# Modulation rows on VectorE behind single up tiles of the feed-forward

## The chip, the cores and the metric

The kernel runs on one core of a Trainium2 chip (trn2). The metric is the device time of one launch in microseconds; the times given are medians over several runs. A profile is one further execution, taken by the hardware profiler; its span runs from the first instruction to the last.

## What is computed

The reference is two layers of a diffusion trunk over 512 latent tokens and 128 context tokens, 1024 features wide. In each layer a conditioning vector (one for the latent tokens, `c`, and one for the context, `c_ctx`) gives six modulation vectors, a mixer with three groups of heads follows, and then a gated feed-forward with a depthwise convolution of width 3 over the tokens:

```python
def _modulation(cvec, w_ada, b_ada):
    m = jax.nn.silu(cvec) @ w_ada + b_ada
    return jnp.split(m[:, None, :], 6, axis=-1)

def _conv_ffn(h, w_ug, conv_w, conv_b, w_down):
    u = h @ w_ug
    ...
    uc = sum(up[:, i:i + n] * conv_w[i] for i in range(CONV_W)) + conv_b
    a, g = jnp.split(uc, 2, axis=-1)
    return (jax.nn.silu(g) * a) @ w_down
```

`w_ug` is 1024 x 5632, `w_down` 2816 x 1024. All is in float32; a product is made of three matmuls on a high and a low part of each factor.

## The kernel before

Features lie on the 128 partitions and the 640 tokens along the free dimension. Each weight tile of 128 x 1024 is loaded (`wr`), split by ScalarE into its high part (`wh`, line 125) and by VectorE into its low part (`wl`, line 188).

The feed-forward (from line 1268 on) has 22 pairs of up tiles. A pair is one tile of the a half and one of the g half. An up tile is 48 matmuls (8 slices of the contraction, 3 products, 2 halves of the tokens, line 278) into one of two wide PSUM accumulators (`Acc`, pool `mm`, two buffers). After a tile, `conv` (line 1278) works on it: VectorE reads the accumulator into `u` (line 1282, two instructions), ScalarE copies the edges (`u`, line 125, two instructions) and these are the last readers of the accumulator; VectorE makes a small `bb` (line 1286), ScalarE the middle tap `y` (line 1289, two instructions), and VectorE adds the other two taps (line 1292, two instructions). For a g tile there follow Silu on ScalarE (line 1306), the product `z` of both halves on VectorE (line 1311), and its split into `th` (ScalarE) and `tl` (VectorE, line 144).

The pairs come in groups of 6, 6, 6 and 4. Behind the first pair of a group stands the down projection of the group before (`dn`, eight chunks of output features). `u["plan"]` holds this order.

The modulation vectors of later use are made in the background, by VectorE: `ada_dve` (line 350 on) is a generator. Its first step loads and prepares the two conditioning vectors (`sbc`); each later step is a row: POOL's queue loads 128 x 1024 weights (`wa`, line 361, two buffers), and VectorE multiplies them with each vector and sums along the row (line 364, two instructions, output `junk`). Layer 0's generator has 48 rows, layer 1's has 8. `CFG[l]["ada"]` says how many steps are taken behind each pair; in the loop over the plan they follow both callbacks (lines 1339 to 1345). In the first three down groups one further step is taken behind each chunk.

Tiles `u`, `y`, `z`, `th`, `tl` and `junk` come from one pool with one tag, S. The framework's planner puts the instructions of each engine in an order before the run: it starts from the order of the program and may move an instruction ahead where it is ready, except where `pin` keeps the order of the program.

Of the kernel before, what the change touches and what calls it, by code (L numbers as in the profile page):

```python
# [32 lines left out]
CFG = [{}, {}]  # L33
# [1 line left out]
CFG[0]["fill"] = (5.5, 6.0, 8.5, 8.5, 5.5, 3.0, 5.5, 9.5, 5.5, 6.5, 8.0, 7.5, 8.5, 11.0, 5.0)  # L35
CFG[0]["early"] = (0.5, 1.0, 1.0, 1.0, 0.7, 0.0, 0.3, 0.7, 1.0, 0.5, 0.3, 1.0, 0.5, 0.3, 0.5)
CFG[0]["mid"] = (0.5, 0.5, 0.2, 0.5, 0.0, 0.5, 0.0, 1.0, 0.5, 0.5, 0.8, 0.0, 0.0, 1.0, 0.0)
CFG[0]["ada"] = (3, 1, 1, 1, 2, 1, 1, 1, 1, 2, 1, 1, 1, 1, 1, 2, 1, 1, 1, 1)
CFG[0]["ahead"] = (8, 4)
CFG[0]["kv"] = 0  # L40
CFG[0]["late"] = ()
# [6 lines left out]
CFG[1]["fill"] = (7.5, 4.5, 4.5, 8.0, 9.0, 4.0, 5.5, 4.5, 5.0, 7.0, 11.5, 10.5, 10.5, 7.5, 5.0)  # L48
CFG[1]["early"] = (1.0, 0.7, 0.5, 0.7, 0.7, 1.0, 0.7, 0.3, 0.5, 0.7, 0.1, 1.0, 1.0, 0.5, 0.3)
CFG[1]["mid"] = (0.5, 0.8, 1.3, 0.0, 0.0, 0.2, 0.2, 0.2, 0.2, 0.0, 0.0, 0.0, 0.0, 0.0, 0.0)  # L50
CFG[1]["ada"] = (3, 1, 2, 1, 2)
CFG[1]["ahead"] = (4, 5)
CFG[1]["kv"] = 7
CFG[1]["late"] = (3,)
# [24 lines left out]
def hybrid_step(ctx: ExitStack, tc: tile.TileContext, I, O):  # L79
# [10 lines left out]
    def S(name, dt=F32, w=NT):  # L90
        return sp.tile([128, w], dt, tag="S", name=name)
# [23 lines left out]
    def SM(name, w=4, bufs=4):  # L115
        return sm.tile([128, w], F32, tag=name, name=name, bufs=bufs)

    def halves(ap):
        return ap.rearrange("p (a b) -> p a b", a=2)
# [4 lines left out]
    def acopy(out, in_):  # L124
        return nc.scalar.activation(out, in_, AF.Copy)  # L125
# [16 lines left out]
    def hilo(hi, lo, src, fix=False):  # L142
        pin(acopy(hi, src), fix)
        nc.vector.tensor_sub(lo, src, f32(hi))
# [55 lines left out]
    for l in range(L):  # L200
# [6 lines left out]
        for n in CFG[l]["order"].split():  # L207
# [6 lines left out]
            elif n[:2] == "po":  # L214
                i = int(n[2])
# [43 lines left out]
    def P(l, n):  # L259
        return pk[l][:, PK[n][0]:PK[n][1]]  # L260
# [972 lines left out]
    if True:  # L1233
# [22 lines left out]
        for l in range(L):  # L1256
            u = U[l]

            def begun():
                x.clear()  # L1260
                i = nc.vector.tensor_scalar_mul(nsink[:, l], P(l, "sink"), -1.0)
                if l:
                    tc.keep_in_program_order(i)

            xn, nrm = mixer(l, nrm, begun, I["xT"] if l == 0 else xd)


            hs = nrm.hs()
            cv = P(l, "conv").rearrange("p (t q) -> p t q", q=4)
            T = {}  # L1270
            bg = ada_dve(0, [(0, n) for n in range(40, 48)] + [(1, n) for n in range(40)]) if l == 0 else ada_dve(48, [(1, n) for n in range(40, 48)])
            made = 0

            nws = SM("nws", 2 * NFT, 1)
            nc.vector.reduce_sum(out=nws, in_=cv[:, :, 0:3], axis=AX.X)
            nc.vector.tensor_scalar_mul(nws, nws, -1.0)

            def conv(ps, t):
                uu = S("u", w=UW)
                for c0, c1, o, p in ((0, NL, 0, 1), (CX, NT, 256, 515)):  # L1280
                    n = c1 - c0
                    nc.vector.tensor_mul(halves(uu[:, p:p + n]), ps.t[:, :, o:o + n // 2], halves(nrm.r[:, c0:c1]))  # L1282
                for v, o in enumerate((uu[:, 0:514:513], uu[:, 514:644:129])):
                    acopy(o, ps.t[:, 1, HF + v:HF + v + 1].to_broadcast([128, 2]))
                bb = SM("bb", 2)
                nc.vector.scalar_tensor_tensor(out=bb, in0=uu[:, 513:515], scalar=nws[:, t:t + 1], in1=cv[:, t, 3:4].to_broadcast([128, 2]), op0=ALU.mult, op1=ALU.add)  # L1286
                y = S("y", w=UW)
                for v, (c0, c1) in enumerate(((0, 513), (513, TW))):
                    nc.scalar.activation(y[:, c0:c1], uu[:, c0 + 1:c1 + 1], AF.Identity, bias=bb[:, v:v + 1], scale=cv[:, t, 1:2])  # L1289
                yy = y[:, :TW]  # L1290
                for q in (0, 2):
                    nc.vector.scalar_tensor_tensor(out=yy, in0=uu[:, q:q + TW], scalar=cv[:, t, q:q + 1], in1=yy, op0=ALU.mult, op1=ALU.add)  # L1292
                return yy

            ya = {}

            def cb_a(f):
                def go(ps):
                    ya[f] = conv(ps, 2 * f)
                return go  # L1300

            def cb_g(f):
                def go(ps):
                    y = conv(ps, 2 * f + 1)
                    a = ya.pop(f)
                    nc.scalar.activation(y, y, AF.Silu)  # L1306
                    if f == NFT - 1:
                        nc.scalar.activation(SM("root", 1, 1), y[:, 1:2], AF.Sqrt, bias=eps[:, 0:1], scale=0.0)
                    z = S("z")
                    for c0, c1, o in ((0, NL, 0), (CX, NT, 2)):  # L1310
                        nc.vector.tensor_mul(z[:, c0:c1], a[:, c0 + o:c1 + o], y[:, c0 + o:c1 + o])
                    T[f] = tuple(S(n, F32R) for n in ("th", "tl"))
                    hilo(T[f][0], T[f][1], z)
                return go

            fin = l == L - 1
            nxt = Norm(xn, None if fin else l + 1, 0)
            if fin:
                yout = {}

                def hfin(hf, c):
                    if c not in yout:
                        yout[c] = S("yo")
                    sl = slice(hf * HF, (hf + 1) * HF)
                    nc.vector.scalar_tensor_tensor(out=yout[c][:, sl], in0=xn[c][:, sl], scalar=P(0, "gfin")[:, c:c + 1], in1=nxt.r[hf][:, :HF], op0=ALU.mult, op1=ALU.mult)  # L1325
                    nc.sync.dma_start(out=O["y"][c, :, sl], in_=yout[c][:, sl])

            def upd_d(last):
                def go(c, ps, hfs):
                    resid(xn[c], ps, l, 5, c, hfs)  # L1330
                    if last:
                        for hf in hfs:
                            nxt.sq(c, hf)
                        if not fin and 1 in hfs:
                            nc.gpsimd.dma_start(out=xd[c], in_=xn[c])
                return go

            for kind, a in u["plan"]:
                if kind == "up":
                    for q, cb in (("a", cb_a(a)), ("g", cb_g(a))):  # L1340
                        ps = Acc()
                        drain(dense(W.get(u[q, a]), hs, range(8), ps, True, True, n=UW))
                        cb(ps)
                    for _ in range(CFG[l]["ada"][a] if a < len(CFG[l]["ada"]) else 0):
                        made += next(bg, 0)
                    continue
                while made < 8:
                    made += next(bg)
                f0, f1 = GROUPS[a]
                nk = f1 - f0  # L1350
                ts = tuple({k: T[f0 + k][q] for k in range(nk)} for q in range(2))
                last = a == len(GROUPS) - 1
                up = upd_d(last)
                if not last:
                    for c in range(8):
                        ps = Acc()
                        drain(dense(W.get(u["d", a, c]), ts, range(nk), ps, True, True))
                        up(c, ps, (0, 1))
                        next(bg, None)
                else:  # L1360
                    drain(bg)
                    accs = [Acc(), Acc(), Acc(False)]
                    for ks in (range(nk - 1), range(nk - 1, nk)):
                        for c in range(3):
                            drain(dense(W.get(u["dl", c // 2]), ts, ks, accs[c], ks[0] == 0, ks[0] != 0, off=(c % 2) * nk))
                            if ks[0]:
                                up(c, accs[c], (0, 1))
                    ps = Acc()
                    drain(dense(W.get(u["dl", 1]), ts, range(nk), ps, True, True, off=nk))
                    up(3, ps, (0, 1))  # L1370
                    items = [(c, W.get(u["dl", c // 2], 3 - c // 4), range(nk), (c % 2) * nk) for c in range(4, 8)]
                    done = 0
                    for i in tail(nxt, items, ts, up):
                        upto = CFG[l]["next"][i]
                        for c in range(done, upto):
                            if fin:
                                hfin(0, c)
                            else:
                                nxt.h(0, c)
                        done = upto  # L1380
                    if fin:
                        nxt.stats(1)
                        for c in range(done, 8):
                            hfin(0, c)
                        for c in range(8):
                            hfin(1, c)
                for f in range(f0, f1):
                    T.pop(f)
            nrm = nxt
# [123 lines left out]
```

## Time and profile before

| | us |
|---|---|
| median of 3 runs | 1578.85 (1576.09 to 1584.0) |
| profiled execution, its own time | 1582.09 |
| its span | 1580.3 |
| TensorE busy | 1525.2 |
| VectorE busy | 1116.7 |
| ScalarE busy | 712.3 |

Times in the profile are microseconds from the start of the span. PE is TensorE, DVE is VectorE, ACT is ScalarE, POOL is GpSimd. L278 is line 278 of the kernel; a name like `u<-mm` is the output and the input by the program's names. A trailing x2 says that two instructions in a row are merged. Idle time in square brackets is followed by what ended it. An instruction can be shown to end after the next one on its engine has begun, so what an instruction takes of its engine is read from start to start.

### The profile page before, as it was taken

What the parts mean: (1) busy time and instruction counts of PE and PEld (TensorE: products, weight loads), DVE (VectorE), ACT (ScalarE), POOL (GpSimd) and SP (SyncE); (2) the same over time, 40 slices, a digit from 0 to 9 for tenths busy, and PEclk for the clock granted to TensorE, in tenths of its full rate; (3) what the DMA queues carried; (4) which work ended last, traced back from release to release, by engine and by line L of the source; (5) the groups of instructions that cost most, each with busy time, mean ns of one, the idle gap of its engine ahead of it and who ended that gap; (6) DMA issues with size and microseconds to landing.
All of it is one profiled execution on the core that took longest, in us unless ns stands there. A gap on an engine that the chain in (4) does not pass through costs nothing. (4 is left out here: it accounts for less than half of the span.)

```text
span 1580.3 us, 25827 instructions
## 1 busy us (share of the span) xinstructions
PE 1525.2 (97%) x10082; PEld 1426.3 (90%) x10082; DVE 1116.7 (71%) x2257; ACT 712.3 (45%) x1403; POOL 103.7 (7%) x225
## 2 busy tenths in 40 slices
PE   9999989899999999999999999989999999999997
PEld 7977775599999999999999887869999999999997
DVE  5765674477897888889778777867885466466366
ACT  4555664564432432441445666646433243244142
POOL 1200111100000000001011000120000000000000
PEclk9999999899999999999999999999999999999998
DMA  9542239113334335235244202331332222221211
GB/s 363 166 145 74 73 98 312 56 54 120 116 124 169 120 104 196 104 104 193 81 142 133 72 25 86 114 142 54 120 99 75 81 74 61 94 77 52 100 54 67
DMA packets 61800, 177.59 MB, mean 112 GB/s; under 512 B 7360, under 2 KB 9856, under 8 KB 61680
## 3 DMA queue, kind: packets, MB, share of 16 engines
q1 hardware_dynamic: 44112, 116.41, 22.1%
q0 software_dynamic: 17568, 59.55, 11.2%
q8 instruction: 79, 1.29, 0.3%
q14 instruction: 41, 0.34, 0.1%
HBM read 165.02 MB, written 10.91 MB: 111 GB/s over the span
## 5 line engine op out<-in xcount | busy, mean ns | idle before, releaser
L278 PE MATMUL mm<-hh,wh 128*128 128x320 f32 x1632 | 377.5, 312 | 12.3 <-ACT u L125 9.1
L278 PE MATMUL mm<-hl,wh 128*128 128x320 f32 x1632 | 377.2, 310 | 0.7 <-DVE hl L486 0.4
L278 PE MATMUL mm<-hh,wl 128*128 128x320 f32 x1632 | 376.9, 310 | 0.0
L125 ACT ACTIVATE wh<-wr 128x1024 fp32r<-128x1024 f32 (+2 forms) x189 | 185.9, 984 | 343.1 <-PE mm L278 263.9
L278 PEld LDWEIGHTS mm<-hh,wh 128*128 128x128 f32 x1632 | 273.8, 188 | 20.6 <-ACT u L125 11.0
L278 PEld LDWEIGHTS mm<-hl,wh 128*128 128x128 f32 x1632 | 275.6, 188 | 4.0 <-issue 2.1
L278 PEld LDWEIGHTS mm<-hh,wl 128*128 128x128 f32 x1632 | 274.5, 188 | 3.3 <-issue 3.3
L188 DVE TENSOR_TENSOR wl<-wr,wh 128x1024 fp32r<-128x1024 f32 (+2 forms) x187 | 210.9, 1128 | 48.2 <-ACT wh L125 47.3
L1292 DVE SCALAR_TENSOR_TENSOR y<-u,pk,y 128x642 f32<-128x642 f32 x176 | 156.2, 887 | 67.9 <-ACT y L1289 64.2
L278 PE MATMUL mm<-th,wh 128*128 128x320 f32 x656 | 152.4, 310 | 0.0
L278 PE MATMUL mm<-th,wl 128*128 128x320 f32 x656 | 152.2, 309 | 0.0
L278 PE MATMUL mm<-tl,wh 128*128 128x320 f32 x656 | 152.0, 309 | 0.0
L537 DVE SCALAR_TENSOR_TENSOR x<-mm,mod,x 128x192 f32<-128x192 f32 (+2 forms) x222 | 84.9, 435 | 70.6 <-PE mm L278 70.6
L364 DVE CUSTOM_DVE_ANT_0 junk<-wa,sbc 128x1024 bf16<-128x1024 f32 x112 | 132.1, 1223 | 1.8 <-DMA wa<-in_wat 1.8
L1289 ACT ACTIVATE y<-u,bb,pk 128x513 f32<-128x513 f32 (+1 forms) x176 | 105.9, 650 | 60.8 <-DVE bb L1286 60.8
L278 PEld LDWEIGHTS mm<-th,wh 128*128 128x128 f32 x656 | 110.3, 188 | 0.7 <-ACT th L125 0.4
L278 PEld LDWEIGHTS mm<-th,wl 128*128 128x128 f32 x656 | 110.4, 188 | 0.0
L278 PEld LDWEIGHTS mm<-tl,wh 128*128 128x128 f32 x656 | 110.4, 188 | 0.0
L1282 DVE TENSOR_TENSOR u<-mm,r 128x512 f32<-128x512 f32 (+1 forms) x176 | 79.6, 486 | 42.2 <-PE mm L278 40.1
L125 ACT ACTIVATE u<-mm 128x2 f32<-128x2 f32 x176 | 20.8, 170 | 112.5 <-DVE u L1282 107.5
L1306 ACT ACTIVATE y<-y 128x642 f32<-128x642 f32 x44 | 32.6, 741 | 73.7 <-DVE y L1292 73.7
L361 POOL DMA_DIRECT2D wa<-in_wat x56 | 29.5, 528 | 524.2 <-DVE mod L364 517.8
(311 smaller groups left out, 2195.6 us busy)
## 6 DMA issues: line engine op xcount, KB each, us to landing
wr<-in_wug SPq DMA_DIRECT2D x88, 512.0 KB, 3.5
wa<-in_wat POOLq DMA_DIRECT2D x56, 512.0 KB, 3.8
wa<-in_wa SPq DMA_DIRECT2D x80, 256.0 KB, 5.7
wr<-in_wdn SPq DMA_DIRECT2D x48, 384.0 KB, 3.1
wr<-in_wi SPq DMA_DIRECT2D x16, 512.0 KB, 3.7
wr<-in_wo SPq DMA_DIRECT2D x14, 512.0 KB, 3.7
xpart<-xp POOLq DMA_DIRECT2D x16, 320.0 KB, 3.7
x<-xpart POOLq DMA_DIRECT2D x16, 320.0 KB, 6.1
```

The source lines that it names most:

```text
L125: return nc.scalar.activation(out, in_, AF.Copy)
L188: pin(self.eng.tensor_sub(lo, r, f32(hi)), fix)
L278: pin(nc.tensor.matmul(ps.h[hf][:, :c1 - c0], lhsT=w[wi][:, off[k] if isinstance(off, dict) else k + off, :], rhs=hs[hi][k][:, c0:c1], sta ...
L361: nc.gpsimd.dma_start(out=t, in_=I["wat"][i0 + i])
L364: nc.vector.tensor_tensor_reduce(out=junk, in0=t, in1=sb[v], scale=1.0, scalar=0.0, op0=ALU.mult, op1=ALU.add, accum_out=mod[l][:, n, v:v ...
L537: nc.vector.scalar_tensor_tensor(out=xc[:, c0:c1], in0=ps.h[hf][:, o:o + c1 - c0], scalar=mod[l][:, gidx * 8 + c, v:v + 1], in1=xc[:, c0:c ...
L1282: nc.vector.tensor_mul(halves(uu[:, p:p + n]), ps.t[:, :, o:o + n // 2], halves(nrm.r[:, c0:c1]))
L1289: nc.scalar.activation(y[:, c0:c1], uu[:, c0 + 1:c1 + 1], AF.Identity, bias=bb[:, v:v + 1], scale=cv[:, t, 1:2])
L1292: nc.vector.scalar_tensor_tensor(out=yy, in0=uu[:, q:q + TW], scalar=cv[:, t, q:q + 1], in1=yy, op0=ALU.mult, op1=ALU.add)
L1306: nc.scalar.activation(y, y, AF.Silu)
```

## The change

The table `ada` now has an entry for each up tile in place of each pair: entry 2a is for the a tile of pair a, entry 2a + 1 for its g tile. An entry of 1 takes one step of the generator behind that tile's callback. The loop over the two tiles counts them with `i`, and the step stands inside that loop. Nothing else differs.

```diff
--- before.py
+++ after.py
@@ -35,7 +35,7 @@
 CFG[0]["fill"] = (5.5, 6.0, 8.5, 8.5, 5.5, 3.0, 5.5, 9.5, 5.5, 6.5, 8.0, 7.5, 8.5, 11.0, 5.0)
 CFG[0]["early"] = (0.5, 1.0, 1.0, 1.0, 0.7, 0.0, 0.3, 0.7, 1.0, 0.5, 0.3, 1.0, 0.5, 0.3, 0.5)
 CFG[0]["mid"] = (0.5, 0.5, 0.2, 0.5, 0.0, 0.5, 0.0, 1.0, 0.5, 0.5, 0.8, 0.0, 0.0, 1.0, 0.0)
-CFG[0]["ada"] = (3, 1, 1, 1, 2, 1, 1, 1, 1, 2, 1, 1, 1, 1, 1, 2, 1, 1, 1, 1)
+CFG[0]["ada"] = (1,) * 12 + (1, 0) * 13
 CFG[0]["ahead"] = (8, 4)
 CFG[0]["kv"] = 0
 CFG[0]["late"] = ()
@@ -48,7 +48,7 @@
 CFG[1]["fill"] = (7.5, 4.5, 4.5, 8.0, 9.0, 4.0, 5.5, 4.5, 5.0, 7.0, 11.5, 10.5, 10.5, 7.5, 5.0)
 CFG[1]["early"] = (1.0, 0.7, 0.5, 0.7, 0.7, 1.0, 0.7, 0.3, 0.5, 0.7, 0.1, 1.0, 1.0, 0.5, 0.3)
 CFG[1]["mid"] = (0.5, 0.8, 1.3, 0.0, 0.0, 0.2, 0.2, 0.2, 0.2, 0.0, 0.0, 0.0, 0.0, 0.0, 0.0)
-CFG[1]["ada"] = (3, 1, 2, 1, 2)
+CFG[1]["ada"] = (1,) * 9
 CFG[1]["ahead"] = (4, 5)
 CFG[1]["kv"] = 7
 CFG[1]["late"] = (3,)
@@ -1337,12 +1337,12 @@
 
             for kind, a in u["plan"]:
                 if kind == "up":
-                    for q, cb in (("a", cb_a(a)), ("g", cb_g(a))):
+                    for i, (q, cb) in enumerate((("a", cb_a(a)), ("g", cb_g(a)))):
                         ps = Acc()
                         drain(dense(W.get(u[q, a]), hs, range(8), ps, True, True, n=UW))
                         cb(ps)
-                    for _ in range(CFG[l]["ada"][a] if a < len(CFG[l]["ada"]) else 0):
-                        made += next(bg, 0)
+                        if 2 * a + i < len(CFG[l]["ada"]) and CFG[l]["ada"][2 * a + i]:
+                            made += next(bg, 0)
                     continue
                 while made < 8:
                     made += next(bg)
```

In layer 0 the old table asked for 25 steps behind pairs 0 to 19 and the new one asks for 25 behind pairs 0 to 18: one behind every tile of pairs 0 to 5, then one behind each a tile of pairs 6 to 18. In layer 1 both ask for 9 behind pairs 0 to 4, the new one behind each of the first nine tiles.

## Rows read from the trace of the kernel before

**Rows 1.** The page, part 1: busy time, share of the span, instructions of each engine

```profile
PE 1525.2 (97%) x10082; PEld 1426.3 (90%) x10082; DVE 1116.7 (71%) x2257; ACT 712.3 (45%) x1403; POOL 103.7 (7%) x225
```

**Rows 2.** TensorE's waits over the whole span: releaser, us in total, times, longest

```profile
PE mm L278 <- ACT u L125: 9.1, 7, 1.4
PE mm L286 <- ACT P L1105: 4.9, 5, 2.0
```

**Rows 3.** The same entry in 340:480, 480:860 and 1100:1200 us, in this order

```profile
PE mm L278 <- ACT u L125: 2.4, 2, 1.4
...
PE mm L278 <- ACT u L125: 2.9, 2, 1.4
...
PE mm L278 <- ACT u L125: 3.9, 3, 1.4
```

**Rows 4.** TensorE's timeline: start us, us, line, op, count [idle before <-releaser]

```profile
371.97 0.45 PE L278 MATMUL mm<-hh,wl 128*128 128x320 f32 x2
373.86 0.57 PE L278 MATMUL mm<-hh,wh 128*128 128x320 f32 x2 [1.44 <-ACT u L125]
```

**Rows 5.** VectorE's timeline behind pair 0 and in pair 1 of layer 0

```profile
367.34 0.82 DVE L144 TENSOR_TENSOR tl<-z,th 128x640 fp32r<-128x640 f32 x1
368.07 1.22 DVE L364 CUSTOM_DVE_ANT_0 junk<-wa,sbc 128x1024 bf16<-128x1024 f32 x1
...
372.65 0.89 DVE L1282 TENSOR_TENSOR u<-mm,r 128x512 f32<-128x512 f32 x2
...
374.72 0.89 DVE L1282 TENSOR_TENSOR u<-mm,r 128x512 f32<-128x512 f32 x2
...
378.37 1.81 DVE L1292 SCALAR_TENSOR_TENSOR y<-u,pk,y 128x642 f32<-128x642 f32 x2 [0.47 <-ACT y L1289]
381.05 0.89 DVE L1311 TENSOR_TENSOR z<-y 128x512 f32<-128x512 f32 x2 [0.87 <-ACT y L1306]
...
383.17 0.82 DVE L144 TENSOR_TENSOR tl<-z,th 128x640 fp32r<-128x640 f32 x1
...
386.20 0.88 DVE L1282 TENSOR_TENSOR u<-mm,r 128x512 f32<-128x512 f32 x2
```

**Rows 6.** ScalarE's timeline, same pairs: splits at tile ends, and a copy of edges

```profile
365.10 1.06 ACT L125 ACTIVATE wh<-wr 128x1024 fp32r<-128x1024 f32 x1 [0.58 <-PE mm L278]
...
372.17 1.06 ACT L125 ACTIVATE wh<-wr 128x1024 fp32r<-128x1024 f32 x1 [5.38 <-PE mm L278]
373.57 0.24 ACT L125 ACTIVATE u<-mm 128x2 f32<-128x2 f32 x2 [0.34 <-DVE u L1282]
...
395.07 1.06 ACT L125 ACTIVATE wh<-wr 128x1024 fp32r<-128x1024 f32 x1 [0.19 <-PE mm L278]
```

**Rows 7.** VectorE's timeline, a pair with one row (pair 3 of layer 0)

```profile
400.33 0.88 DVE L1282 TENSOR_TENSOR u<-mm,r 128x512 f32<-128x512 f32 x2
401.58 0.22 DVE L1286 SCALAR_TENSOR_TENSOR bb<-u,nws,pk 128x2 f32<-128x2 f32 x1 [0.36 <-ACT u L125]
...
404.87 0.22 DVE L1286 SCALAR_TENSOR_TENSOR bb<-u,nws,pk 128x2 f32<-128x2 f32 x1
...
406.36 1.81 DVE L1292 SCALAR_TENSOR_TENSOR y<-u,pk,y 128x642 f32<-128x642 f32 x2
```

**Rows 8.** Busy time in a one-row pair: stretch, length, DVE busy, PEclk, DMA share, GB/s

```profile
387.45:401.58 14.13, 11.74 (x20) 1.00 0.32 113
```

**Rows 9.** VectorE's timeline, pair 0 of layer 0, no row yet

```profile
356.73 1.81 DVE L1292 SCALAR_TENSOR_TENSOR y<-u,pk,y 128x642 f32<-128x642 f32 x2 [1.27 <-ACT y L1289]
358.45 0.88 DVE L1282 TENSOR_TENSOR u<-mm,r 128x512 f32<-128x512 f32 x2
359.25 1.22 DVE L188 TENSOR_TENSOR wl<-wr,wh 128x1024 fp32r<-128x1024 f32 x1
```

**Rows 10.** POOL's row loads: the first two in its timeline; landing of all 56

```profile
302.26 1.05 POOL L361 DMA_DIRECT2D wa<-in_wat  x2 [1.58 <-PE mm L286]
...
DMA to landing us min/median/max: 3.6/3.8/7.9
```

## The prediction

> **What bounds the kernel now.** The page comes first. TensorE is busy for 97% of the span and VectorE for 71% [rows 1], so the end is set by TensorE's work plus the few places where TensorE waits. The next view is therefore the list of TensorE's waits. Its largest entry is 9.1 us in 7 waits for ScalarE's `u` copies [rows 2], the last instruction that reads an up tile's PSUM accumulator. Cut by stretch, that entry is 2 waits in 340 to 480 us, 2 in 480 to 860 and 3 in 1100 to 1200 [rows 3]. The old tables ask for two rows behind a pair (a "3" is the set-up and two rows) at pairs 0, 4, 9 and 15 of layer 0 and at pairs 0, 2 and 4 of layer 1. That is four places and three, one for each wait.
>
> The timelines show how such a wait arises. TensorE's stream breaks off at 372 us and goes on at 373.86 [rows 4]. On VectorE, `tl` of pair 0 stands at 367.34, four row instructions follow from 368.07, and only at 372.65 is the next a accumulator read [rows 5], after which ScalarE copies its edges at 373.57 [rows 6]. There are two accumulators, so the tile after next can't start before that read. A row (two instructions, one for each conditioning vector) takes 2.29 us: the lump of two is 372.65 - 368.07 = 4.58.
>
> The profile prints less than such a wait costs, since a matmul's modelled end lies after the next one's normal start. ScalarE's `wh` splits start at tile ends and give the true loss: 365.10 to 372.17 is one tile, 7.07 us, and 372.17 to 395.07 is 22.90 [rows 6], three tiles and 1.69. The idle time shown there was 1.44 [rows 4], so I add 0.25 to each wait: 9.1 + 7 x 0.25 = **10.85 us** lost to the lumps. A lump of one row causes no wait, and the second row, 2.29, causes 1.69, so a one-row pair has 0.60 us to spare. A pair of tiles is 14.14 us of TensorE.
>
> **What the change moves.** The number of rows is the same: 25 steps (the set-up and 24 rows) in layer 0 over pairs 0 to 18, 9 steps in layer 1. Afterwards pair 0 has the set-up behind a and one row behind g. Pairs 1 to 5 of layer 0 and 1 to 3 of layer 1 have a row behind each tile. Pairs 6 to 18, and pair 4 of layer 1, have one row behind a. No pair has two rows in one place, so all seven waits as they stand now go: **-10.85 us**. In exchange eight pairs of two rows follow one another, five and three, where before every two-row pair had a one-row pair or a down group behind it. The 8 rows of each down group stay where they are.
>
> **What the two-row pairs cost.** A one-row pair has VectorE busy for 11.74 of 14.13 us [rows 8]; a second row makes 14.03. So TensorE's 14.14 is met only if VectorE hardly ever waits inside a pair, and each half of a pair has a chain through ScalarE. Where can a row stand? Its data can be there early: the first two row loads went out at 302.26 [rows 10], yet VectorE sat idle for 1.27 us before a `y` at 356.73 [rows 9] and the row was not put there but behind `tl`. I read this as the planner taking the pool tiles of tag S (`u`, `y`, `z`, `th`, `tl`, `junk`) in program order, and use it for the new order. A row behind a then comes as soon as `y` of a has its tile, that is after `bb`, and fills that idle time; `u` of g has to stay behind it; and a row behind g still comes after `tl`.
>
> With start-to-start times from the trace such a pair runs:
> - a half: `u`, `wl` and `bb` take 374.72 - 372.65 = 2.07 [rows 5], the row 2.29 (ScalarE's `y` runs under it), the two `y` steps 358.45 - 356.73 = 1.72 [rows 9]. Sum 6.08.
> - g half: `u` takes 359.25 - 358.45 = 0.80 [rows 9], `bb` to the first `y` step 406.36 - 404.87 = 1.49 [rows 7], from there to `tl`, with a `wl` in it, 383.17 - 378.37 = 4.80 [rows 5], `tl` 368.07 - 367.34 = 0.73, the row 2.29. Sum 10.11.
>
> That is **16.19 us**, 2.05 more than TensorE's pair. The bounds: if every wait is covered, 14.03 and nothing is lost. If `u` of g is not tucked between the two `y` steps of a, the wait behind it is open: `u` to `bb` is 401.58 - 400.33 = 1.25 [rows 7] in place of 0.80, and the pair takes 16.64. Nearest of what was run is the pair behind a lump, 386.20 - 372.65 = 13.55 with one row [rows 5], which makes 15.84 with two. I take 16.19, as all of it but the place of the rows is seen.
>
> Eight pairs give 8 x 2.05 = 16.4, less 0.60 to spare at the start of each layer: 15.2. At the end of the stretch in layer 0 comes the first down group. Its chunk 0 (36 matmuls of 7.07 / 48 us) takes 5.3 us in place of 7.07, and chunk 1 wants the accumulator that `u` of g frees 6.08 + 1.2 = 7.3 us after `u` of a, while chunk 0 ends 1.2 + 5.3 = 6.5 after it: **+0.8**. The 1.2 is from the read at 372.65 to the restart at 373.86 [rows 4, 5].
>
> Things costed at nothing: one-row pairs with the row behind a come to 16.19 - 2.29 = 13.90, within 14.14. The row loads move with the rows; a buffer is asked for again only after two rows, about 16.2 - 2.3 = 13.9 us, and the slowest landing is 7.9 [rows 10], so if that cover went the cost would be a few waits at most. POOL's queue holds nothing else there, and SP's weight loads keep their order. `wl`, pushed back by a row, makes weights that are not the next tile's, and no wait for them shows in these stretches [rows 3].
>
> **Sum:** -10.85 + 15.2 + 0.8 = **+5.2 us**. The profiled execution took 1582.09 us, 1.8 of it outside the span, and would be 1587.3; it lies 3.2 above the median of the runs shown. From the median, 1578.85 + 5.2 = **1584.0 us**.
>
> **The rivals.** A measurement of this kernel can tell about 0.5% from no change, 7.9 us: 1571.0 to 1586.7.
>
> A, *the waits simply go.* If the planner's order covers the chains (`wl` in one gap, rows in the others), 14.03 fits into 14.14 and -10.85 stays: 1568.0. For it: VectorE's 83% in a one-row pair [rows 8], and the lump being the only thing ahead of the late read. Against it: 0.11 us of room a pair, and a chain behind `u` of g that no row may enter. Chance 0.2, with part of it short of the full gain.
> The Trainium skill has this as a rule: in Perfetto Trace Analysis, section Optimizing Scalar/DVE Operations, it says that where Vector isn't saturated but causes bubbles on other engines, breaking up instructions may let work be done sooner. By that rule the time would be A's; the trace agrees as to the bubbles, but at 14.03 of 14.14 its condition is no longer met in the eight pairs.
>
> B, *the rows don't part.* The planner could leave the row of a to stand beside that of g, so the change would not do what it says: eight pairs at 15.84, 8 x 1.70 - 1.2 - 10.85 = +1.5: 1580.4. Against it: `u` of g comes later in the program than the row and uses the same pool. Chance 0.15.
>
> C, *the g half stays open.* Because the row of a holds back `u` of g, nothing covers the copies behind it, and every pair takes 16.64: 8 x 2.50 - 1.2 + 0.8 - 10.85 = +8.8: 1587.6, slower. It decides from a pair of about 16.5 us on. For it: the wait from `u` to `bb` is in the one-row pairs too [rows 7]. Against: there `u` of g mostly comes before the last `y` step. Chance 0.15.
>
> **How the numbers follow.** The forecast has 0.5 and reaches from +2 to +8. A gives about 0.16 of faster by over 0.5%, C and the upper end of the forecast 0.22 of slower, and 0.62 is left for within 0.5%. The range of 1570 to 1590 leaves out most of A and the end of C.
>
> **What would show it.** Right: the seven `u` waits of 1.0 to 1.4 us are gone at pairs 9 and 15 of layer 0; in pairs 1 to 5 (some 358 to 445 us) and in layer 1 from 1108 to 1160 TensorE waits for `u` once a pair, about 2 us each, some 13 us in all; row instructions stand between `bb` and `y` of a, and VectorE is busy over 85% there. Wrong: no `u` waits in these stretches (A), four row instructions still in a line (B), or a time moved outside the feed-forward, which nothing above accounts for.

## The result, and the profile after

The changed kernel takes 1590.4 us in the median of 12 runs (1585.01 to 1597.04); the kernel before, run beside it 12 times, takes 1581.48. The ratio is **1.0063 with an interval of 1.005 to 1.0077**: slower, by 8.9 us. The forecast was +5.2 us, and 1590.4 lies just outside its range of 1570 to 1590. The sign was right, and so was the mechanism in the main; a size was wrong. The forecast of 1584.0 was missed by 6.4 us: by 3.7 in what the change costs, and by 2.6 because the kernel before itself took 1581.48 in these 12 runs and 1578.85 in the 3 that the forecast was built on. On that base 8.9 us more would have been 1587.8, inside the range, so it is in part chance that the range was missed.

The page, part 1, of the changed kernel, and below it the view of the core with its span and its mean granted clock. Its profiled execution took 1597.04 us, the longest of the 12.

```profile
PE 1531.5 (96%) x10082; PEld 1430.4 (90%) x10082; DVE 1115.0 (70%) x2257; ACT 713.9 (45%) x1403; POOL 103.4 (6%) x225
```

```profile
core 0: 1594.9 us, clock 0.980
```

Against [rows 1] the counts of instructions are the same, and VectorE is busy no longer. TensorE's busy time has grown by 6.3 us with not one matmul more: some of them ran slower. The other new time lies in TensorE's waits. Their largest entry over the whole span, and then the same entry in 365 to 462, 462 to 490 and 1140 to 1240 us (us in total, times, longest):

```profile
PE mm L278 <- ACT u L125: 15.8, 10, 3.1
```

```profile
PE mm L278 <- ACT u L125: 9.3, 5, 3.1
...
PE mm L278 <- ACT u L125: 0.8, 1, 0.8
...
PE mm L278 <- ACT u L125: 5.7, 4, 1.8
```

These answer to [rows 2, 3]. The three stretches hold all ten waits. The same list from 490 to 860 us has no such entry, so the waits behind pairs 9 and 15 of layer 0 are gone. In the stretches with two-row pairs TensorE now waits once a pair, for 0.8 to 3.1 us, where it had waited for 1.0 to 1.4 us in one pair out of two to six. The next view is VectorE's timeline in pairs 1 and 2 of layer 0 (start, duration, line, operation, count, idle before and releaser):

```profile
372.75 0.89 DVE L1282 TENSOR_TENSOR u<-mm,r 128x512 f32<-128x512 f32 x2
...
389.03 0.88 DVE L1282 TENSOR_TENSOR u<-mm,r 128x512 f32<-128x512 f32 x2
...
390.96 0.21 DVE L1286 SCALAR_TENSOR_TENSOR bb<-u,nws,pk 128x2 f32<-128x2 f32 x1
391.09 1.22 DVE L364 CUSTOM_DVE_ANT_0 junk<-wa,sbc 128x1024 bf16<-128x1024 f32 x1
...
393.38 0.89 DVE L1292 SCALAR_TENSOR_TENSOR y<-u,pk,y 128x642 f32<-128x642 f32 x1
394.18 0.69 DVE L1282 TENSOR_TENSOR u<-mm,r 128x512 f32<-128x512 f32 x1
394.78 0.88 DVE L1292 SCALAR_TENSOR_TENSOR y<-u,pk,y 128x642 f32<-128x642 f32 x1
...
396.23 0.22 DVE L1286 SCALAR_TENSOR_TENSOR bb<-u,nws,pk 128x2 f32<-128x2 f32 x1 [0.36 <-ACT u L125]
397.72 1.81 DVE L1292 SCALAR_TENSOR_TENSOR y<-u,pk,y 128x642 f32<-128x642 f32 x2 [1.27 <-ACT y L1289]
399.45 1.22 DVE L188 TENSOR_TENSOR wl<-wr,wh 128x1024 fp32r<-128x1024 f32 x1
...
402.28 0.83 DVE L144 TENSOR_TENSOR tl<-z,th 128x640 fp32r<-128x640 f32 x1 [0.81 <-ACT th L125]
403.02 1.22 DVE L364 CUSTOM_DVE_ANT_0 junk<-wa,sbc 128x1024 bf16<-128x1024 f32 x1
...
405.31 0.88 DVE L1282 TENSOR_TENSOR u<-mm,r 128x512 f32<-128x512 f32 x2
```

The rows have parted as laid out: one between `bb` and `y` of a, the other behind `tl`, with `u` of g tucked in between the two `y` steps of a. From read to read of the a accumulator a pair takes 389.03 - 372.75 = **16.28 us**, and 405.31 - 389.03 = 16.28 again, where 16.19 was forecast. The g half of pair 2 has three open waits for ScalarE, 0.36 before `bb`, 1.27 before `y` and 0.81 before `tl`. Read the same way, the five two-row pairs of layer 0 take 16.28, 16.28, 16.77, 17.62 and 18.08 us (pairs 1 to 5), and those of layer 1 take 16.29, 16.29 and 16.28, with 15.77 for the one-row pair behind them. So the pair is as costed at first, and then it grows.

Two things stand where it grows. The first is the clock. TensorE's timeline (start, duration, count) at the wait behind pair 2, and the stretch around it (length, busy times of PE, PEld, DVE, ACT and POOL, PEclk, DMA share, GB/s):

```profile
404.20 0.45 PE L278 MATMUL mm<-hh,wl 128*128 128x320 f32 x2
406.51 0.56 PE L278 MATMUL mm<-hh,wh 128*128 128x320 f32 x2 [1.87 <-ACT u L125]
...
408.12 0.74 PE L278 MATMUL mm<-hl,wh 128*128 128x320 f32 x2
408.66 0.74 PE L278 MATMUL mm<-hh,wl 128*128 128x320 f32 x2
...
410.81 0.46 PE L278 MATMUL mm<-hh,wh 128*128 128x320 f32 x2
411.11 0.46 PE L278 MATMUL mm<-hl,wh 128*128 128x320 f32 x2
```

```profile
406.00:412.00 6.00, 5.49 (x27) 5.49 (x28) 6.00 (x11) 1.44 (x4) 0.74 (x2) 0.72 0.68 201
```

TensorE stands still for 1.87 us, goes on at full speed, and a good 1 us later two matmuls take 408.66 - 408.12 = 0.54 us from start to start in place of 411.11 - 410.81 = 0.30: the lower of its two levels, 1.2 GHz in place of 2.4. From 410.81 on it is back. The granted clock of 0.72 over 6 us says the same: 0.28 x 6 = 1.7 us lost. The clock's record shows three such falls of 3.4 us in the feed-forwards of this execution, at waits of 1.9, 3.1 and 1.8 us (the granted clock is 0.57 from 441 to 445 us and from 1182 to 1186 us too); two other waits of 1.8 and 2.1 us had none. In the trace of before, whose u waits are all 1.4 us or less [rows 2], there is none in the feed-forwards.

The second is the order on VectorE. Its timeline in pair 5:

```profile
446.64 0.22 DVE L1286 SCALAR_TENSOR_TENSOR bb<-u,nws,pk 128x2 f32<-128x2 f32 x1 [0.36 <-ACT u L125]
448.13 0.89 DVE L1292 SCALAR_TENSOR_TENSOR y<-u,pk,y 128x642 f32<-128x642 f32 x1 [1.27 <-ACT y L1289]
450.42 0.96 DVE L188 TENSOR_TENSOR wl<-wr,wh 128x768 fp32r<-128x768 f32 x1 [1.40 <-ACT wh L125]
451.30 0.88 DVE L1292 SCALAR_TENSOR_TENSOR y<-u,pk,y 128x642 f32<-128x642 f32 x1
453.05 0.90 DVE L1311 TENSOR_TENSOR z<-y 128x512 f32<-128x512 f32 x2 [0.87 <-ACT y L1306]
```

In pairs 4 and 5 the planner's fixed order has a `wl` between the two `y` steps of g. With `wl` there, nothing is left to cover the wait of `z` for Silu, 0.87. In pair 5 this `wl` also waits 1.40 us for ScalarE's `wh`, which needs a buffer (four of them) that comes free when TensorE ends a tile. That tile had run into the fall of the clock at 441 us: it took 449.64 - 440.91 = 8.7 us in place of 7.2. So what the clock takes from TensorE makes VectorE late, and VectorE's late read makes TensorE late again. In pairs 3 and 4, behind the fall at 407 us, a `wl` waits 0.40 and 0.31 us for `wh` in the same way. Run e8 below tells the order and the clock apart.

Outside these stretches little has moved. The first `u` of layer 0 stands at 355.37 against 352.98 us, so 2.4 of the 14.6 us between the two spans are there before the first instruction of the change. The pairs account for 11.2 of the other 12.2: 4.1 over the forecast in layer 0, 1.9 in layer 1, and the forecast 5.2.

### The profile page after: what moved, and what is told of

It reads as the page before. It is cut to its first block, busy times and chain, and to the rows that moved or that the text cites. A ratio compares the mean times of both kernels' runs of the same rounds, so it can differ in the third digit from the quotient of the medians.

```text
span 1594.9 us, 25842 instructions
## 1 busy us (share of the span) xinstructions
PE 1531.5 (96%) x10082; PEld 1430.4 (90%) x10082; DVE 1115.0 (70%) x2257; ACT 713.9 (45%) x1403; POOL 103.4 (6%) x225
## 3 DMA queue, kind: packets, MB, share of 16 engines
q8 instruction: 79, 1.29, 0.3%
## 5 line engine op out<-in xcount | busy, mean ns | idle before, releaser
L537 DVE SCALAR_TENSOR_TENSOR x<-mm,mod,x 128x192 f32<-128x192 f32 (+2 forms) x222 | 84.6, 435 | 75.5 <-PE mm L278 75.5
L1306 ACT ACTIVATE y<-y 128x642 f32<-128x642 f32 x44 | 32.6, 740 | 68.5 <-DVE y L1292 68.5
```

The source lines that it names most:

```text
L537: nc.vector.scalar_tensor_tensor(out=xc[:, c0:c1], in0=ps.h[hf][:, o:o + c1 - c0], scalar=mod[l][:, gidx * 8 + c, v:v + 1], in1=xc[:, c0:c ...
```

## The experiments

The theory: a row behind each tile leaves the g half's waits for ScalarE open, so a two-row pair costs 16.3 us against TensorE's 14.14; many in a row bring waits at every pair, and the longer of these bring the clock down. The rival: the split rows are harmless, and the time is lost elsewhere (in how many rows follow one another, in the clock alone, or outside the feed-forward).

**e1: two-row pairs far apart.** Same kernel, other table.

```diff
-CFG[0]["ada"] = (1,) * 12 + (1, 0) * 13
+CFG[0]["ada"] = (1, 1) + (1, 0) * 2 + (1, 1) + (1, 0) * 3 + (1, 0) * 7 + (1, 1) + (1, 0) * 7
-CFG[1]["ada"] = (1,) * 9
+CFG[1]["ada"] = (1, 1) + (1, 0) * 2 + (1, 1) + (1, 0) * 3
```

> Same steps, but the two-row pairs no longer follow one another: in layer 0 the 25 steps are spread over all 22 pairs (one behind each a tile, a second one only at pairs 3 and 14; pair 0 has the set-up and one row), in layer 1 a second row only at pair 3. Theory 1 (VectorE needs about 16.3 us for a pair with two rows, TensorE 14.14, and the lag of pairs in a row adds up): a two-row pair behind one-row pairs has 2.9 us to spare and costs nothing, so hardly any of the u waits is left and the kernel is some 11 us faster than the kernel before (ratio about 0.993). Rival (a row behind an a tile is itself the trouble, since the read of the g accumulator has to stay behind it): the u waits stay, one at nearly every pair that has a row behind a, and the time is at or above that of the changed kernel (ratio 1.006 or more).

Measured: 1.0002 (0.999 to 1.0015). Neither expectation came true: the gain of 0.7% is missing, and so are the rival's waits at nearly every pair. Part of the reason is in TensorE's waits (total, times, longest):

```profile
PE mm L278 <- ACT u L125: 6.6, 8, 1.0
```

The two-row pair 3 of each layer (16.27 and 16.28 us) is followed by four waits. A pair with one row behind a takes 13.98 us undisturbed, only 0.16 less than TensorE, and the next two take 14.8 to 14.9: a `wl` stands between the `y` steps of g, which leaves `z` open, and while TensorE is late `wl` waits up to 0.56 us for `wh`, here without a fall of the clock. The lag is not worked off. The two-row pair 14 of layer 0 (16.57 us) has pairs of 13.98, 13.82 and 13.55 us behind it, and no wait follows. Besides, with rows behind the last pairs TensorE waited 2.8 us for `diag` in the layer's tail, where the kernel before waits 0.2. So a lag lasts until something with less work on VectorE comes.

**e2: the same numbers of steps, but both rows of a pair behind its g tile.** The kernel before with the changed kernel's counts.

```diff
-CFG[0]["ada"] = (3, 1, 1, 1, 2, 1, 1, 1, 1, 2, 1, 1, 1, 1, 1, 2, 1, 1, 1, 1)
+CFG[0]["ada"] = (2,) * 6 + (1,) * 13
-CFG[1]["ada"] = (3, 1, 2, 1, 2)
+CFG[1]["ada"] = (2, 2, 2, 2, 1)
```

> The loop of the kernel before, with as many rows in each pair as the changed kernel has (two steps behind pairs 0 to 5 of layer 0 and 0 to 3 of layer 1, then one), but both behind the g tile. Theory 1: the number of rows in pairs that follow one another decides, not their place; a pair takes 15.84 us on VectorE, TensorE waits about 1.7 us at each of eight pairs, 12.4 us in all against the 10.85 of the kernel before: ratio 1.001, up to 1.004 if its clock falls behind a wait as it does in the changed kernel. Rival (place): without a row behind a it runs like a kernel without the trouble, 0.995 or less.

Measured: 1.0001 (0.9989 to 1.0014). Its waits, and two reads of the a accumulator one pair apart on VectorE:

```profile
PE mm L278 <- ACT u L125: 10.6, 8, 1.4
```

```profile
399.45 0.88 DVE L1282 TENSOR_TENSOR u<-mm,r 128x512 f32<-128x512 f32 x2
...
415.29 0.88 DVE L1282 TENSOR_TENSOR u<-mm,r 128x512 f32<-128x512 f32 x2
```

The pair takes 415.29 - 399.45 = 15.84 us, the price of rival B to the hundredth, and eight waits of 1.4 us or less, with no fall of the clock behind any, cost the time nothing that can be measured against the kernel before. That is what theory 1 expected (1.001). With equal counts of rows per pair, the changed kernel is 0.6% slower. So two rows in each of these pairs cost no more than the lumps of before, and what is slower is where they stand: the row behind a costs 16.28 - 15.84 = 0.44 us a pair more than the same row behind g. Eight pairs of that are 3.5 us; that the rest of the difference is the growth of the pairs and the clock is read from the traces and not shown by this run.

**e3 and e4: a shorter row.** The changed kernel, with the second of a row's two VectorE instructions over 512 (e3), and over 64 (e4), of its 1024 columns; both leave out part of the sums. The edit of e4:

```diff
-                    out=junk, in0=t, in1=sb[v], scale=1.0, scalar=0.0, op0=ALU.mult, op1=ALU.add,
+                    out=junk[:, :64 if v else 1024], in0=t[:, :64 if v else 1024], in1=sb[v][:, :64 if v else 1024], scale=1.0, scalar=0.0, op0=ALU.mult, op1=ALU.add,
```

> The changed kernel with the second vector's sum of each row taken over 512 of 1024 columns, so a row takes about 1.75 us in place of 2.29 (part of the computation is left out). Theory 1: a two-row pair takes 16.28 - 1.07 = 15.2 us on VectorE, TensorE loses about 1.07 at each of eight pairs less the 1.2 to spare, some 7.5 us, against 10.85 before: ratio about 0.998, if the clock no longer falls behind waits of about 0.8 us. If the clock falls all the same: three falls of 1.5 us more, ratio 1.001. Rival (place): ratio as the changed kernel, 1.006.

> The changed kernel with the second vector's sum of each row taken over 64 of 1024 columns, so a row takes about 1.3 us (part of the computation is left out). Theory 1: a two-row pair takes 14.3 us, the u waits go nearly all, ratio about 0.993 to 0.994. Rival (place, that is the order in which the read of the g accumulator stands behind a row): waits remain at each pair and the ratio is over 1.0.

Measured: 1.0015 (1.0002 to 1.0028) with 512 columns and 0.9946 (0.9929 to 0.9964) with 64. Their waits, in this order:

```profile
PE mm L278 <- ACT u L125: 9.6, 9, 2.0
```

```profile
PE mm L278 <- ACT u L125: 1.1, 1, 1.1
```

With 64 columns the waits of the split rows nearly go: 1.1 us is left of 9.1 [rows 2], and 8.5 us are gained. With 512 they stay, since the pair takes 15.4 to 16.4 us and not the 15.2 expected (in two of the pairs a `wl` waits 0.8 and 1.0 us for `wh`), and the clock falls once. So VectorE's time in the pair is the cause of the waits. How much of the 0.5% is due to the placing is not shown: the kernel before was not run with the short row, which takes 1.29 us in e4. A lump of two, 2.58, is less than the 2.29 + 0.60 that by the prediction's count cause no wait, so its waits might have gone without any placing.

**e5: one row in nearly every pair, behind its g tile.** The changed kernel with counts in the table.

```diff
-CFG[0]["ada"] = (1,) * 12 + (1, 0) * 13
+CFG[0]["ada"] = (2, 1) + (0, 1) * 6 + ((1, 1) + (0, 1) * 5) * 2 + (1, 1)
-CFG[1]["ada"] = (1,) * 9
+CFG[1]["ada"] = (2, 1) + (0, 1) * 6
...
-                        if 2 * a + i < len(CFG[l]["ada"]) and CFG[l]["ada"][2 * a + i]:
+                        for _ in range(CFG[l]["ada"][2 * a + i] if 2 * a + i < len(CFG[l]["ada"]) else 0):
```

> No pair has two rows in one place, and nearly every pair has just one, behind its g tile: in layer 0 pair 0 has the set-up and a row behind a and a row behind g, pairs 1 to 6 one behind g, pairs 7, 13 and 19 (the first behind a down group) one behind each tile, the others to 18 one behind g; layer 1 as layer 0 to pair 6. Theory 1 (the load of a pair on VectorE decides, 13.55 us with a row behind g, 13.98 with a row behind a, 15.84 to 16.28 with two, against 14.14 on TensorE): the long run of u waits goes; a wait of at most 0.6 us is left at pair 0 of each layer, and the time is some 9 to 10 us below the kernel before, ratio about 0.994. Rival (the waits are bound to the number of rows in the first seven pairs, which is the same): ratio 1.0.

**e6: pairs with a row behind each tile, and pairs with none, in turn.** The changed kernel's loop.

```diff
-CFG[0]["ada"] = (1,) * 12 + (1, 0) * 13
+CFG[0]["ada"] = (1, 1, 0, 0) * 2 + (1, 1, 1, 0, 1, 1) + (1, 1, 1, 0, 1, 1, 0, 0) + (1, 1, 1, 0) + (1, 1, 0, 0) * 4
-CFG[1]["ada"] = (1,) * 9
+CFG[1]["ada"] = (1, 1, 0, 0) * 2 + (1, 1, 1, 0, 1, 1)
```

> The form of the changed kernel (a row behind a and one behind g), but a pair with two rows is followed by a pair with none or one: ten such pairs in layer 0 between pairs 2 and 19, three in layer 1. Theory 1 (the lag of pairs in a row is what TensorE pays): a two-row pair takes 16.28 us, 2.14 too many; behind an empty pair VectorE reads the next accumulator about 2.9 us before TensorE needs it, so most of them cost nothing; one wait of about 1.2 us is left at pair 6 of each layer, ratio about 0.995. Rival (every pair with a row behind each tile costs TensorE about 2 us): ten to thirteen waits, ratio 1.005 or more.

Measured: 1.0048 (1.003 to 1.0067) for e5 and 1.0046 (1.0029 to 1.0063) for e6. Both missed 0.994 to 0.995 by a whole per cent, and the waits say much of why (e5 first, then e6):

```profile
PE mm L278 <- DVE x L537: 8.2, 3, 4.6
PE mm L278 <- ACT u L125: 5.4, 6, 1.0
```

```profile
PE mm L278 <- DVE x L537: 12.2, 3, 6.7
PE mm L278 <- ACT u L125: 1.1, 1, 1.1
```

In e6 the u waits fell to a single one, as the theory has it: up to pair 4 its pairs alternate between 11.8 and 16.1 to 16.5 us, so a lone two-row pair costs nothing where the next one can make up for it. The one wait stands behind pair 9, where the pair before has a row too. In e5 they fell less than expected, to six of up to 1.0 us where one of 0.6 a layer was to be left: its pairs 1 to 4 take 13.9, 15.6, 13.9 and 15.1 us, not 13.55, and in the longer ones a `wl` waits 0.82 and 0.58 us for `wh`. But a wait that the trace of before has at 0.3 us became the longest. VectorE's timeline of e6 at layer 0's first down group, and what TensorE waited for there:

```profile
457.30 0.17 DVE L370 TENSOR_TENSOR mod<-mod,pk 128x16 f32<-128x16 f32 x1
457.39 1.22 DVE L364 CUSTOM_DVE_ANT_0 junk<-wa,sbc 128x1024 bf16<-128x1024 f32 x1
...
458.53 2.17 DVE L537 SCALAR_TENSOR_TENSOR x<-mm,mod,x 128x320 f32<-128x320 f32 x6
```

```profile
459.81 0.87 PE L278 MATMUL mm<-th,wh 128*128 128x320 f32 x2 [6.68 <-DVE x L537]
```

The residual of a down chunk (L537) takes the gate out of `mod`, which is whole only when eight rows are made and the bias is added (L370). In both kernels the ninth step (the set-up is the first) came behind pair 6, not pair 5, so the gate was late and the down group stood for it. This is the constraint that the old table's two rows at pairs 0 and 4 serve: nine steps by pair 5. So e6 misses for a reason of its own, and e5 in part; e6 still shows what the theory says of lone pairs.

**e7: three rows in one place.** The kernel before with longer lumps.

```diff
-CFG[0]["ada"] = (3, 1, 1, 1, 2, 1, 1, 1, 1, 2, 1, 1, 1, 1, 1, 2, 1, 1, 1, 1)
+CFG[0]["ada"] = (4, 1, 1, 1, 3, 0, 1, 1, 0, 3, 0, 1, 1, 1, 0, 3, 0, 1, 1, 1, 1)
-CFG[1]["ada"] = (3, 1, 2, 1, 2)
+CFG[1]["ada"] = (4, 0, 1, 1, 3)
```

> The kernel before with lumps of three rows behind g (pairs 0, 4, 9, 15 of layer 0, pairs 0 and 4 of layer 1), the steps taken from other pairs. Six waits of 1.44 + 2.29 = 3.7 us in place of seven of 1.3, so 23.7 us lost in place of 10.85: +12.9, ratio 1.008, if the price of a wait is its length. If a wait of over about 1.8 us also brings the granted clock down for one stretch of 3.4 us behind it, as at three places of the changed kernel, where the tile behind the wait takes 8.6 us in place of 7.07: six times 1.5 us more, +22, ratio 1.014, and the record of the granted clock has falls in the feed-forward, which the kernel before has not.

Measured: 1.024 (1.0209 to 1.0271), more than either expectation. The waits are longer than 3.7 us: behind pair 0 the third row starts 1.8 us after the second has ended, since its load goes out at 370.08, when the first row has freed one of the two `wa` buffers, and takes at least 3.7 us to land. The wait list, TensorE's timeline at the first of them, and the 10 us from there on:

```profile
PE mm L278 <- ACT u L125: 32.6, 6, 5.6
```

```profile
377.31 0.90 PE L278 MATMUL mm<-hh,wh 128*128 128x320 f32 x2 [5.55 <-ACT u L125]
```

```profile
377.31:387.31 10.00, 9.99 (x50) 10.00 (x51) 7.34 (x12) 4.27 (x9) 0.00 (x0) 0.71 0.19 58
```

At each of the six waits the clock's record has one fall of 6.8 us, twice as long as those of the changed kernel. It begins while TensorE still stands (the first two matmuls behind the wait take 0.90 us, where at 406.51 above they take 0.56), and only what is left of it costs time: 0.29 x 10 = 2.9 us in the stretch shown. The same stretch behind the other five waits has a granted clock of 0.69 to 0.79; all six together lose 16.3 us. That comes on top of the waits themselves, 32.6 less the 9.1 of before; together 40, and the medians differ by 38. The clock is a cost of its own beside the wait that brings it, and it was in no sum of mine.

**e8: the change in layer 0 alone.** The changed kernel with layer 1's steps placed as before (the loop as in e5).

```diff
-CFG[1]["ada"] = (1,) * 9
+CFG[1]["ada"] = (1, 2) + (0, 1) + (0, 2) + (0, 1) + (0, 2)
```

> Layer 0 as in the changed kernel, layer 1 with its rows where the kernel before has them. By the waits and the clock of the two profiles layer 0 lost 6.3 us to u waits before and 12.6 + 0.8 with about 3 us of slow clock after, so layer 0 alone should give about +7 of the some +9 us: ratio 1.0045. If the two layers share it by their two-row pairs (five and three) without a term of the clock, about +4: 1.0025.

Measured: 1.0057 (1.0037 to 1.0077), which takes in the first expectation and not the second. Nearly all of the 1.0063 is layer 0's; what is left for layer 1 can't be told from nothing. The profiled execution had no fall of the clock in the feed-forward, though TensorE stopped for 1.3 to 2.8 us behind each pair of layer 0. TensorE at the longest of these stops, the 6 us behind it, and VectorE in pair 5:

```profile
436.99 0.57 PE L278 MATMUL mm<-hh,wh 128*128 128x320 f32 x2 [2.80 <-ACT u L125]
```

```profile
437.00:443.00 6.00, 6.00 (x40) 6.00 (x41) 5.58 (x11) 1.46 (x5) 0.53 (x1) 1.00 0.70 223
```

```profile
444.21 0.89 DVE L1292 SCALAR_TENSOR_TENSOR y<-u,pk,y 128x642 f32<-128x642 f32 x1 [1.27 <-ACT y L1289]
445.02 0.95 DVE L188 TENSOR_TENSOR wl<-wr,wh 128x768 fp32r<-128x768 f32 x1
445.89 0.88 DVE L1292 SCALAR_TENSOR_TENSOR y<-u,pk,y 128x642 f32<-128x642 f32 x1
447.64 0.89 DVE L1311 TENSOR_TENSOR z<-y 128x512 f32<-128x512 f32 x2 [0.87 <-ACT y L1306]
```

The `wl` that waited 1.40 us in the changed kernel does not wait here, nor does any other in these pairs. The five pairs take 16.28, 16.29, 16.28, 17.22 and 16.58 us: in the last two `wl` stands between the `y` steps and `z` is open, and pair 4 also has the step that adds the bias to `mod` (L370). So of the growth in layer 0 the order makes 82.65 - 5 x 16.28 = 1.25 us. The other 85.03 - 82.65 = 2.4 us of the changed kernel came with its two falls, most of it as the three waits of `wl` for `wh` (0.40, 0.31, 1.40). This sets one execution against one; e10 below has the two falls and the changed kernel's pair times again.

**e9: the change only where no step is due soon.** Before's places up to pair 5 and in layer 1, e6's alternation from pair 7 on.

```diff
-CFG[0]["ada"] = (1,) * 12 + (1, 0) * 13
+CFG[0]["ada"] = (1, 2) + (0, 1) * 3 + (0, 2) + (0, 1) + (0, 0) + (1, 1, 1, 0, 1, 1, 0, 0) + (1, 1, 1, 0) + (1, 1, 0, 0) * 4
-CFG[1]["ada"] = (1,) * 9
+CFG[1]["ada"] = (1, 2) + (0, 1) + (0, 2) + (0, 1) + (0, 2)
```

> The kernel of before up to pair 5 of layer 0 and in layer 1 (9 steps by pair 5, two rows in one place at pairs 0 and 4; layer 1 untouched), and the form of the alternating table from pair 7 on (a row behind each tile of a pair, then a pair with none), where no later step needs the rows soon. The u waits at pairs 9 and 15 (1.4 and 1.4 us, lost 2.9 + 2 x 0.25 = 3.4) go and the five others stay: theory (an isolated pair with parted rows costs TensorE nothing) u waits about 6.3 us in 5, ratio 0.998. Rival (what was lost there was hidden further on, at the start of the down groups or the tail): the same waits, but ratio 1.000, with a longer wait at L537 or L383 in their place.

Measured: 1.0 (0.9985 to 1.0015). The waits:

```profile
PE mm L278 <- ACT u L125: 7.4, 6, 1.4
```

The wait behind pair 15 went, and that behind pair 9, where the pair before has a row too, is 1.1 us in place of 1.4. So 1.7 us of 9.1 are saved in the list, 0.1% of the time, which the interval can't tell from nothing. Neither expectation is confirmed: the ratio is the rival's, but its longer wait at L537 or L383 is not there. It was the candidate to beat both kernels; it beats the changed one and ties with the one before.

**e10: twelve pairs of two rows.** Layer 0's 25 steps all behind consecutive tiles, layer 1 as before (the loop as in e5).

```diff
-CFG[0]["ada"] = (1,) * 12 + (1, 0) * 13
+CFG[0]["ada"] = (1,) * 25
-CFG[1]["ada"] = (1,) * 9
+CFG[1]["ada"] = (1, 2) + (0, 1) + (0, 2) + (0, 1) + (0, 2)
```

> The changed kernel with all 25 steps of layer 0 one behind each tile of pairs 0 to 12, and layer 1 as before: six more two-row pairs, 6 to 11, behind the first down group, and no row from pair 13 on. It tells whether a pair with parted rows has a constant time or one that grows with the lag. Constant at 16.28: five more pairs behind the down group at 16.28 - 14.14 = 2.14 each, less 0.6, +10.1 us on the 1.0057 of the kernel with the change in layer 0 alone: 1.012. Growing as in pairs 3 to 5 of the first stretch (+0.6, +1.4, +1.9) with one or two more falls of the clock (1.7 us each): +15.5 to 17.5 us, 1.0155 to 1.017, with periods near 17 at pairs 9 to 11 and u waits over 2 us there.

Measured: 1.0139 (1.012 to 1.0158), between the two, with an interval that reaches from one to the other, so the pairs have to decide. Its waits, and on VectorE the reads of the a accumulator that begin and end pairs 9 to 11, behind the first down group:

```profile
PE mm L278 <- ACT u L125: 23.6, 15, 3.1
```

```profile
545.90 0.88 DVE L1282 TENSOR_TENSOR u<-mm,r 128x512 f32<-128x512 f32 x2
...
562.18 0.88 DVE L1282 TENSOR_TENSOR u<-mm,r 128x512 f32<-128x512 f32 x2
...
579.03 0.88 DVE L1282 TENSOR_TENSOR u<-mm,r 128x512 f32<-128x512 f32 x2
...
595.61 0.88 DVE L1282 TENSOR_TENSOR u<-mm,r 128x512 f32<-128x512 f32 x2
```

Pairs 8 to 11 take 16.44, 16.28, 16.85 and 16.58 us: neither constant at 16.28 nor growing towards 18. In the two longer ones the `wl` stands between the `y` steps of g, and `z` waits 0.87 for ScalarE; in the others it stands behind them. So the pair moves between 16.3 and 16.9 with the place of a `wl`, and the 17.6 and 18.1 of the changed kernel need more: there `wl` waited for `wh` behind a fall of the clock. In this run's own pairs 1 to 5, with falls at 405 and 440 us, the times are those of the changed kernel to 0.02 us, the wait of 1.40 before `wl` included. Each of the four pairs again has a wait of 1.9 to 2.4 us; one 3.4 us fall of the clock stands among them.

## Why the prediction was wrong

**Right: what bounded the kernel, and what goes.** TensorE's waits for `u` were the lumps of two rows. Where the new table has one row a pair, they are gone (490 to 860 us), and nothing else came in their place there.

**Right: where the rows go on VectorE.** The order from the planner's program order held to the instruction, `u` of g between the two `y` steps included (its large part; the small one behind them). Two sizes in pair 2 differ from the layout. From the first `y` of a to `bb` of g it takes 396.23 - 393.38 = 2.85 us against 1.72 + 0.80, since the copies behind `u` of g are open by 0.36. From the `y` steps of g to `tl` it takes 402.28 - 397.72 = 4.56 against 4.80. The two nearly cancel, 16.28 against 16.19, so that the price was met to 0.1 us is in part luck. One sign was missed: VectorE is busy for 81% of pairs 1 to 5 in layer 0 and 85% in layer 1, not over 85%, as it waits too.

**The step that failed: "Eight pairs give 8 x 2.05 = 16.4, less 0.60 to spare at the start of each layer: 15.2."** It takes the pair to be as long at the eighth time as at the first, whatever TensorE does meanwhile. Measured, layer 0's five pairs take 85.03 us where 5 x 16.19 = 80.95 was costed, and layer 1's three 48.86 against 48.57, with a one-row pair of 15.77 behind them where 14.14 was costed. That is 6.0 us more in the profiled execution, which took 6.6 us above the median.

**What it left out, first: the place of `wl`.** The words "no wait for them shows in these stretches" were said of its weights and taken as a reason to cost it at nothing. That looked at TensorE's waits alone, and TensorE does not wait for these weights after the change either. But the layout took one order for all pairs, and in pairs 4 and 5 of layer 0 `wl` stands between the `y` steps of g and leaves `z` open: 1.25 us by e8, with no fall of the clock. And `wl` can wait for `wh` when TensorE ends a tile late, which then makes the pair of VectorE longer: in these pairs that came behind the falls of the clock (2.4 us in layer 0), in e1 without one. e10 shows that the pairs don't build up without bound.

**What it left out, second: the clock.** I took a wait to cost its own length and a quarter of a microsecond. The time of a run times one less its mean granted clock is what the lower level cost it: in the median 26.2 us over the 12 runs of the changed kernel, and 20.5 to 23.7 over 74 runs of the kernel before, beside the experiments. The rest, the time multiplied by the clock, is 1563.7 us against 1557.0 to 1558.0, so by this estimate 5.7 to 6.7 us are waits, near the +5.2 of the sum, and what is left of the 8.9, 2 to 3 us, is clock. The estimate is rough, since the medians of the clock's part differ by 2.5 to 5.7 and some of the lower level falls where TensorE stands anyway. It agrees with e8, whose profiled execution, with no fall in the feed-forward, took 1585.67 us, 6.7 above the median of the kernel before, 1579.01. The profiled execution of the changed kernel, at 0.980, had 32 us of it, which is why it was the longest of the 12. The Trainium skill says in Perfetto Trace Analysis, section Matmul Optimizations, that the matmul engine scales power with its utilization, and that matmuls should run back to back. The trace agrees as far as it goes: in e7 each of six waits of 5.1 to 5.6 us had its fall, and e2's eight of up to 1.4 us had none; e8's five of 1.3 to 2.8 us behind its two-row pairs had none either.

**The rivals.** B's price of 15.84 was exact, but its case did not occur; e2 had to be made for it. C's 1587.6 is the nearest of the four times, and its +8.8 is the +8.9 measured, in part by luck. Its wait behind `u` of g is open in pairs 2, 3 and 5 (0.36), but what C priced, 16.64 in every pair, did not come: the first pairs take 16.28, and the longer ones without a fall (17.22 and 16.58 in e8, 16.85 and 16.58 in e10) have the wait of `z` open, which C did not name. A failed by what was said against it, 14.03 us of work in 14.14: in e4, with shorter rows, the split rows have one wait left.

**Not settled:** why a fall of the clock follows one wait of 1.8 or 2.1 us and not another, nor one of 2.8 us in e8; how many falls the executions without a trace had; and what a fifth buffer for `wh` and `wl` would give back, which was not tried.

## What to carry to other kernels

Where a helper engine's work fills all but 1% of the bound engine's time in a stretch, spreading it evenly turned a few waits into one per iteration here; a lump followed by a lighter iteration cost less, since the lag is worked off. Before moving work, write down which later step needs it whole and by when (here nine steps by pair 5): in e5 and e6 TensorE waited 8.2 and 12.2 us for that. And cost a wait of TensorE by what follows it too: the clock behind it, and the buffers that its late end holds back from the engine that it waits for.

## What the runs showed of the hardware

A short stop of TensorE was at times dearer than its length. Behind a stop of 1.87 us the granted clock went from 2.4 to 1.2 GHz about 1 us after the matmuls had resumed, for 3.4 us, and 1.7 us were lost; at the six stops of 5.1 to 5.6 us in e7 it went down before the matmuls resumed, for 6.8 us, and 2.1 to 3.1 us were lost at each. Of the stops for `u` of up to 1.4 us in the kernel before and in e2 none was followed by a fall. Between 1.8 and 2.1 us both happened, in one and the same execution of the changed kernel, and in e8 four stops of 1.9 to 2.8 us had no fall.
